# A transformer block on one Trainium2 core: a third seven-product pair in both column groups of the product behind the mixers, and a residual that enters the second group through PSUM

## The chip, the core and the metric

One Trainium2 chip, of which the kernel uses one core. The metric is the device time of one execution in microseconds (us), lower is better. The kernel is one launch and works in fp32; matrix products are made from split operands, as told below.

## The reference, cut to what matters

One layer on 256 rows of 2048 features. Two mixers, each with eight heads, work on one input projection; their results `y_sb` and `y_ca` go through a projection each, are gated and summed, and then comes the product that this document is about, `merged @ w_mix_out` with a residual. A gated feed-forward part (FFN) and a small gated addition follow.

```python
merged = (sigmoid(gate_sb) * (y_sb @ w_sb_out[i])
          + sigmoid(gate_ca) * (y_ca @ w_ca_out[i]))
x = x + merged @ w_mix_out[i]          # 256x2048 @ 2048x2048
h = rmsnorm(x, g_ffn[i])
g_ff, u_ff = split(h @ w_ffn_in[i], 2)
x = x + (silu(g_ff) * u_ff) @ w_ffn_out[i]
h = rmsnorm(x, g_ple[i])
x = x + sigmoid(h @ w_ple_gate[i]) * (p[i] @ w_ple_in[i])
out = rmsnorm(x, g_final)
```

## The kernel before, in words

**Split products.** Every operand of a product is held as two numbers, a rounded `hi` and the rest `lo`. A product of two 128-wide blocks is three matmuls of 128x512: hi by hi, hi by lo, lo by hi (`three`, L302 to 307). Activations lie in tables (T1, T2, T3), one 128-row block `kt` of features after the other, hi and lo halves behind each other. Weights come by DMA in pieces of 128x1024 (`raw`, issued by SP, L241); ScalarE (ACT) casts them to `hi` (L277), VectorE (DVE) subtracts to get `lo` (L257). There are five `raw` buffers, and two more from the place told below on; three buffers for `hi` and three for `lo`, later four.

**Units.** The product behind the mixers is made in two units (`unit`, L174), each of 16 feature blocks by two column blocks of 512: the first makes columns 0 to 1023, the second columns 1024 to 2047. In a unit the feature blocks go two and two, pair 0 to pair 7. A plain pair is two pieces, one for each column block, with 12 matmuls each, 24 in all. A pair named in `MIX_PAIRS` is one piece of 21 matmuls instead (`pair_products`, L312): seven products in place of eight, as in Strassen's and Winograd's scheme, on sums of the operands. Four of the seven go to banks of their own (`su`, the other half of PSUM); `mid` (L848) adds these up after the last such pair of a unit.

**What a seven-product pair needs.** Its weights are both column blocks' pieces at once. DVE makes three sums into `xf` and one in place in `raw` (four subtractions of 128x512), ACT casts `xf` to its hi half, DVE subtracts to get its lo half (128x1536); both halves lie in a room of T3 (`mix_rooms`). That is `split_pair` (L282). On the other side it needs a "form", four sums of 128x128 blocks of the table with hi and lo (`sums_of`, L462), made while the table is made; two forms fit in the tile FP.

**What comes ahead.** The two projections behind the mixers go before, on T2, which holds `y_sb` in its blocks 0 to 7 and `y_ca` in 8 to 15. When a column block of the second projection is complete, its gated sum (in `gates`) is transposed on TensorE (PE) and written to T1, four feature blocks at a time (`into_table`, L473). The last of these four steps runs when the first unit is already three pieces in. Then the memory of the attention stage is given up (`att.close`, `mid_stack.close`, L1007 and 1008), T3 and the two added `raw` buffers take the same place, and the four PSUM banks of the attention stage become the `su` banks of the first unit.

**After a unit.** `add_to_residual` (L962) adds, for each of the four 128x512 parts, PSUM to the sums from `mid`, and the result to the residual `x`: two DVE steps each. Units of the FFN's second product have another way, a `seed`: ACT copies the residual into the unit's PSUM banks before its first matmul (`seed_next`, L340), the matmuls accumulate on it, and one DVE step for each part writes `x` (`add_to_sums`, L1064).

**Order.** Each engine works its own instructions strictly in the program's order, which a scheduling layer fixes when the kernel is built. Pieces are split up to three ahead of the products. Whoever stands in an engine's order behind an instruction that waits, waits too.

Of the kernel before, what the change touches and what calls it, by code (L numbers as in the profile page):

```python
# [12 lines left out]
ALU = mybir.AluOpType  # L13
# [5 lines left out]
NT = 2  # L19
D = 2048  # L20
KD = D // P
# [10 lines left out]
NB = 512  # L32
# [1 line left out]
FF_BLOCKS = [12, 16, 16]  # L34

PAIRS = (2, 4, 6)
MIX_PAIRS = (4, 6)
OUT_PAIRS = {12: (2, 3, 4), 16: (2, 4, 5, 6)}
OUT_ORDERS = {
    12: ((0, 0, 1, 1, -2, 3, 3, -4, 5, 5), (0, 0, -2, 1, -3, 1, -4, 5, 5)),  # L40
# [12 lines left out]
def block_kernel(ctx: ExitStack, tc: tile.TileContext, x, p, w_in, w_sb_out, w_ca_out, w_mix_out,  # L53
# [18 lines left out]
    nc = tc.nc  # L72
# [13 lines left out]
    def aux(name):  # L86
        pool, width, tag = ps_ax[-1]
        return pool.tile([P, width], F32, tag=tag, name=name)
# [8 lines left out]
    T1 = bp.tile([P, KD, 2, S], F32R, tag="T1", name="T1")  # L97
    T2 = bp.tile([P, KD, 2, S], F32R, tag="T2", name="T2")
    x_ = bp.tile([P, NT, D], F32, tag="x", name="x")
    FP = bp.tile([P, 2, 2, 4, P], F32R, tag="FP", name="FP")  # L100
# [59 lines left out]
    def group(kind, wsrc, n0, kts, lhs, post, needs=lambda kt: None, row0=0, keep=None, after=None):  # L160

        ncol, nk = (NB, 2) if kind == "row" else (FB, 4)
        g = dict(kind=kind, post=post, lhs=lhs, ps=None, keep=keep, after=after)
        kts = list(kts)
        for j in range(0, len(kts), nk):
            part = kts[j : j + nk]
            r = (row0 + j) * P
            pieces.append(dict(
                g=g, kts=part, ncol=ncol, first=j == 0, last=j + nk >= len(kts),
                src=[wsrc[r : r + len(part) * P, n0 : n0 + ncol].rearrange("(k p) n -> p k n", p=P)],  # L170
                needs=[k for k in (needs(kt) for kt in part) if k is not None],
            ))

    def unit(wsrc, n0s, kts, lhs, forms, ext, slots, mid, post, needs, row0=0, pairs=PAIRS, alone=None, after=None,  # L174
             order=None, seed=None):


        if alone is None:
            state["unit"] = state.get("unit", -1) + 1
        pool = state["unit"] % 2 if alone is None else alone  # L180
        g = dict(kind="unit", post=post, mid=mid, slots=slots, after=after, lhs=lhs, keep=None, forms=forms, ext=ext, pool=pool,
                 side=1 - pool, hold=alone is not None, seed=seed)
        kts = list(kts)
        if order is None:
            order = [j for i in range(len(kts) // 2) for j in ([-i] if i in pairs and i < len(kts) // 2 - 1 else [i, i])]
        taken = [-i for i in order if i < 0]
        begun = set()
        for i in order:
            own = i < 0
            i = abs(i)  # L190
            part = kts[2 * i : 2 * i + 2]
            r = (row0 + 2 * i) * P
            src = [wsrc[r : r + 2 * P, n0 : n0 + NB].rearrange("(k p) n -> p k n", p=P) for n0 in n0s]
            pc = dict(g=g, kts=part, ncol=NB, needs=[needs(kt) for kt in part])
            if own:
                pieces.append(dict(pc, src=src, pair=True, first=i == taken[0], last=i == taken[-1]))
            else:
                b = int(i in begun)
                begun.add(i)
                pieces.append(dict(pc, src=[src[b]], block=b, first=i == 0, last=2 * i + 2 == len(kts)))  # L200
# [229 lines left out]
    def later(fn, n=3):  # L430

        for _ in range(n):
            tasks.append((None, lambda: None))
        tasks.append((None, fn))
# [38 lines left out]
    def into_table(dst, c, src, gain=None, key=None, forms=None, pool=None, pairs=PAIRS):  # L473


        n = ps_ax[-1][1] // S if pool is None else 2
        for k0 in range(0, 4, n):
            ps = (aux("tp") if pool is None else late["ps"][pool].tile([P, 512], F32, tag="mm", name="tp"))
            ps = ps.rearrange("p (k s) -> p k s", k=n)
            for k in range(n):  # L480
                for t in range(NT):
                    nc.tensor.transpose(ps[:, k, t * P : (t + 1) * P], src[:, t, (k0 + k) * P : (k0 + k + 1) * P], ident)  # L482
            step = n if forms is None else 2
            for k1 in range(0, n, step):
                table_part(dst, 4 * c + k0 + k1, ps[:, k1 : k1 + step, :], gain, forms, pairs)
        for k in range(4):
            done.add((key, 4 * c + k))

    def table_part(dst, kt, ps, gain, forms, pairs):
        n = ps.shape[1]  # L490
        ks = slice(kt, kt + n)
        g = None if gain is None else [gT[:, gain + kt + k : gain + kt + k + 1] for k in range(n)]
        if forms is not None and kt // 2 in pairs:
            af = state["work"]("af").rearrange("p (k s) -> p k s", k=2)
            if g is None:
                nc.scalar.copy(af, ps)
            else:
                for k in range(2):
                    nc.scalar.activation(af[:, k, :], ps[:, k, :], AF.Identity, scale=g[k])
            nc.scalar.copy(dst[:, ks, 0, :], af)  # L500
            minus(dst[:, ks, 1, :], af, dst.bitcast(F32)[:, ks, 0, :])
            sums_of(af, forms(kt))
        elif g is None:
            nc.scalar.copy(dst[:, ks, 0, :], ps)
            minus(dst[:, ks, 1, :], ps, dst.bitcast(F32)[:, ks, 0, :])
        else:
            for k in range(n):
                nc.scalar.activation(dst[:, kt + k, 0, :], ps[:, k, :], AF.Identity, scale=g[k])
                nc.vector.scalar_tensor_tensor(dst[:, kt + k, 1, :], ps[:, k, :], g[k], dst.bitcast(F32)[:, kt + k, 0, :],
                                               ALU.mult, ALU.subtract)  # L510
# [404 lines left out]
    x_ = bp.tile([P, NT, D], F32, tag="x", name="x")  # L915
# [7 lines left out]
    def out_post(m, c):  # L923
        def post(ps):
            cs = slice(c * NB, (c + 1) * NB)
            gt = gates[:, :, m, cs]
            for t in range(NT):
                by = rstd if (m, c) == (1, 0) else r1
                with tc.issue_after(state["cast"].ins):
                    nc.scalar.activation(gt[:, t, :], gt[:, t, :], AF.Sigmoid, scale=by["mix"][:, t : t + 1])  # L930
            for t in range(NT):
                nc.vector.tensor_tensor(gates[:, t, m, cs], ps[t], gates[:, t, m, cs], ALU.mult)
            if m == 1:
                mg = gates[:, :, 0, cs]
                nc.vector.tensor_tensor(mg, mg, gt, ALU.add)
                later(lambda: into_table(T1, c, mg, key="mg", forms=lambda kt: FP[:, kt // 4 - 2], pairs=MIX_PAIRS))
        return post

    for m, wo in ((0, w_sb_out), (1, w_ca_out)):
        for c in range(4):  # L940
            group("row", wo[0], c * NB, range(8 * m, 8 * m + 8), T2, out_post(m, c), needs=lambda kt: ("y", kt))
        state["places"] = 0
        flush(2.67 if m == 0 else 1, in_turn=m == 0)
# [13 lines left out]
    def C_slots():  # L957
        C = late["pool"].tile([P, 4, NB], F32, tag="C", name="C")
        late["C"] = C
        return [C[:, i, :] for i in range(4)]  # L960

    def add_to_residual(g, b, c):  # L962
        add_sums(g, b)
        for t in range(NT):
            xc = x_[:, t, c * NB : (c + 1) * NB]
            nc.vector.tensor_tensor(xc, xc, g["C"][2 * b + t], ALU.add)
# [10 lines left out]
    def mix_post(c0):  # L977
        def post(g, b):
            c = c0 + b
            add_to_residual(g, b, c)  # L980
            if b == 1:
                next_tables(late["T3"], c, 16, "ffn", g["pool"])
            residual_done(c, "ffn")
            if c == 3:
                tasks.append(("p2", lambda: broadcast(p2bc, p2, late["pool"])))
        return post
# [14 lines left out]

    mix_rooms = []
    for c in (0, 2):
        unit(w_mix_out[0], (c * NB, (c + 1) * NB), range(KD), T1, lambda kt: FP[:, kt // 4 - 2], mix_rooms, C_slots,
             mid, mix_post(c), lambda kt: ("mg", kt), pairs=MIX_PAIRS)
    flush(until=("mg", KD - 1))
    att.close()  # L1007
    mid_stack.close()
# [42 lines left out]
    def in_post(dst, c, key, pairs):  # L1051
# [8 lines left out]
            if b == 1:  # L1060
                hidden(dst, c, key, g, pairs)
        return post

    def add_to_sums(g, b, c):  # L1064
        for t in range(NT):
            nc.vector.tensor_tensor(x_[:, t, c * NB : (c + 1) * NB], g["ps"][2 * b + t], g["C"][2 * b + t], ALU.add)

    def residual_of(c0):
        return lambda b, t: x_[:, t, (c0 + b) * NB : (c0 + b + 1) * NB]

    def out_unit_post(c0, last):
        def post(g, b):
# [18 lines left out]
    for blk, nk in enumerate(FF_BLOCKS):  # L1091
        key = f"h{blk}"
        for c in range(nk // 4):
# [3 lines left out]
                 pairs=PAIRS if j else (), after=None if j else scale_next)  # L1097
# [124 lines left out]
```

## Time and profile before

| | us |
|---|---|
| median of 3 runs (1456.23 to 1456.53) | 1456.28 |
| the profiled execution, as a run | 1455.66 |
| its span in the profile | 1453.9 |
| PE busy in the span | 1443.5 |
| DVE busy | 1249.7 |
| ACT busy | 829.6 |

The span runs from the first to the last instruction; the run's time lies 1.8 us above it. Lines of the profile name the source line of the kernel before, the engine, the operation, and the tiles as output<-inputs. Matmuls overlap in the engine's pipeline, so that each has a duration of about 0.39 us but a new one starts every 0.23 us; the chain of waits shows the latter. The first of the two units runs from about 569 to 613 us, the second to about 657 us.

### The profile page before, as it was taken

Reading aid. Unit: us, or ns where it says so; the run is one execution under the profiler, and the core shown is the slowest. Engines: PE = TensorE matmul, PEld = TensorE weight load, DVE = VectorE, ACT = ScalarE, POOL = GpSimd, SP = SyncE. Lnnn points to the kernel's source line nnn. Section 1 sums busy time; section 2 is a strip of 40 time slices with the busy share of each in tenths; the row PEclk is TensorE's granted clock in tenths of the full one; section 3 lists DMA queues with packets and bytes.
Section 4 is the critical chain, followed back from the end, with each engine's and each line's share of the span. In section 5 each row is a group of like instructions: output and inputs, shape, how many; then the busy total and the mean of one; then the engine's idle time right before and its main releaser. Section 6 shows DMA issues by size and latency. Waiting matters only on the chain.

```text
span 1453.9 us, 18702 instructions
## 1 busy us (share of the span) xinstructions
PE 1443.5 (99%) x6837; PEld 1208.8 (83%) x6837; DVE 1249.7 (86%) x1587; ACT 829.6 (57%) x993; POOL 25.1 (2%) x44
## 2 busy tenths in 40 slices
PE   9999999999999999999999999999999999999997
PEld 7888888888888888888888888888888888888886
DVE  6979777898987767888999999999999989999785
ACT  6456555655545665555556655566655556666652
POOL 0200000000010000000000000000000000000100
PEclk9999999999999999999999999999999999999999
DMA  9866555666675655765666666666666666665871
GB/s 319 283 189 212 181 172 172 180 205 198 199 257 164 180 168 181 231 204 173 198 192 189 196 222 194 199 201 208 193 194 216 195 186 201 215 189 178 275 230 70
DMA packets 164731, 291.17 MB, mean 200 GB/s; under 512 B 9024, under 2 KB 42096, under 8 KB 164384
## 3 DMA queue, kind: packets, MB, share of 16 engines
q1 hardware_dynamic: 162528, 281.32, 62.0%
q0 software_dynamic: 2112, 8.68, 1.8%
q8 instruction: 53, 0.87, 0.2%
q14 instruction: 38, 0.31, 0.1%
HBM read 284.19 MB, written 5.77 MB: 199 GB/s over the span
## 4 chain that ended last, share of the span: by engine, by line
PE 96%; DVE 2%; DMA 1%; issue 1%; ACT 0%; DVEq 0%; SPq 0%; ACTq 0%
PE mm L307 67%; PE su L307 13%; PE mm L392 8%; PE mm L394 4%; PE tp L482 1%; DVE lo L257 1%; DMA raw<-in_w_in 1%; PE mml L307 0%; DMA raw<-in_w_ple_in 0%; PE mm L382 0%; PE xps L536 0%; DVE xf L257 0%; PE yp L709 0%; ACT hi L277 0%; PE wt L800 0%
## 5 line engine op out<-in xcount | busy, mean ns | idle before, releaser
L307 PE MATMUL mm<-hi,T 128*128 128x512 f32 x2650 | 854.6, 391 | 0.4 <-DVE v L854 0.4
L257 DVE TENSOR_TENSOR lo<-raw,hi 128x1024 fp32r<-128x1024 f32 (+1 forms) x517 | 625.1, 1221 | 121.9 <-ACT hi L277 113.0
L277 ACT CAST hi<-raw 128x1024 fp32r<-128x1024 f32 (+1 forms) x379 | 396.7, 1050 | 381.0 <-PE mm L307 257.8
L307 PEld LDWEIGHTS mm<-hi,T 128*128 128x128 f32 x2650 | 497.3, 188 | 103.0 <-issue 0.8
L307 PE MATMUL mm<-lo,T 128*128 128x512 f32 x1325 | 517.1, 391 | 0.0
L307 PEld LDWEIGHTS mm<-lo,T 128*128 128x128 f32 x1325 | 248.9, 188 | 50.7
L392 PE MATMUL mm<-T,hi 128*128 128x512 f32 x512 | 179.8, 398 | 0.0
L394 PE MATMUL mm<-T,lo 128*128 128x256 f32 x512 | 139.7, 280 | 0.0
L295 ACT CAST hi<-raw 128x1024 fp32r<-128x1024 f32 x69 | 72.7, 1053 | 76.2 <-DVE raw L257 29.5
L257 DVE TENSOR_TENSOR T<-xf,T 128x1536 fp32r<-128x1536 f32 x61 | 107.2, 1757 | 8.0 <-ACT T L298 7.2
L392 PEld LDWEIGHTS mm<-T,hi 128*128 128x128 f32 x512 | 94.6, 188 | 20.1
L257 DVE TENSOR_TENSOR xf<-raw 128x512 f32<-128x512 f32 x138 | 95.1, 689 | 13.2 <-DMA raw<-in_w_ffn_out 4.1
L394 PEld LDWEIGHTS mm<-T,lo 128*128 128x128 f32 x512 | 96.7, 189 | 2.3
L298 ACT CAST T<-xf 128x1536 fp32r<-128x1536 f32 x61 | 90.2, 1479 | 12.7 <-DVE xf L257 12.3
L292 ACT CAST hi<-raw 128x1024 fp32r<-128x1024 f32 x69 | 72.6, 1052 | 31.0 <-PE mm L307 20.5
L307 PE MATMUL mm<-T,T 128*128 128x512 f32 (+1 forms) x279 | 77.2, 371 | 0.0
L307 PE MATMUL su<-hi,T 128*128 128x512 f32 x170 | 66.1, 394 | 0.0
L307 PEld LDWEIGHTS mm<-T,T 128*128 128x128 f32 x279 | 49.3, 188 | 9.1
L854 DVE TENSOR_TENSOR C<-su,C 128x512 f32<-128x512 f32 x72 | 47.8, 686 | 0.4
L257 DVE TENSOR_TENSOR xf<-raw,xf 128x512 f32<-128x512 f32 x69 | 47.5, 689 | 0.5
L257 DVE TENSOR_TENSOR raw<-raw 128x512 f32<-128x512 f32 x69 | 47.5, 689 | 0.4
L307 PE MATMUL su<-T,FP 128*128 128x512 f32 x174 | 47.3, 389 | 0.0
(280 smaller groups left out, 1242.7 us busy)
## 6 DMA issues: line engine op xcount, KB each, us to landing
raw<-in_w_ffn_in SPq DMA_DIRECT2D x176, 512.0 KB, 4.1
raw<-in_w_in SPq DMA_DIRECT2D x160, 512.0 KB, 4.4
raw<-in_w_ffn_out SPq DMA_DIRECT2D x88, 512.0 KB, 4.4
raw<-in_w_mix_out SPq DMA_DIRECT2D x32, 512.0 KB, 4.6
raw<-in_w_ple_gate SPq DMA_DIRECT2D x32, 512.0 KB, 4.9
raw<-in_w_sb_out SPq DMA_DIRECT2D x16, 512.0 KB, 3.8
raw<-in_w_ca_out SPq DMA_DIRECT2D x16, 512.0 KB, 4.5
x<-in_x SPq DMA_DIRECT2D x4, 512.0 KB, 10.2
```

What stands on the lines that cost most here:

```text
L257: return nc.vector.tensor_tensor(out, a, b, ALU.subtract)
L277: state["cast"] = nc.scalar.copy(hi[:, c : c + m], raw[:, c : c + m])
L292: nc.scalar.copy(h1, raw1)
L295: nc.scalar.copy(h2, raw2)
L298: nc.scalar.copy(xh, xf)
L307: state["mm"] = nc.tensor.matmul(ps, u, v, start=first, stop=last, skip_group_check=True)
L392: nc.tensor.matmul(ps, hi[:, i, f], lhs[:, kt, :, :].rearrange("p c s -> p (c s)"), start=a, stop=False)
L394: nc.tensor.matmul(ps[:, :S], lo[:, i, f], lhs[:, kt, 0, :], start=False, stop=z)
L482: nc.tensor.transpose(ps[:, k, t * P : (t + 1) * P], src[:, t, (k0 + k) * P : (k0 + k + 1) * P], ident)
L854: nc.vector.tensor_tensor(C[i], q, C[j], ALU.add)
```

## The change

Pair 2 becomes a seven-product pair in both units (`MIX_PAIRS`). Its form needs a third place, and lies where T2 holds the blocks 0 and 1 of `y_sb`, which only the first projection reads (`F_mix`). The second unit is seeded with the residual, so that `add_to_sums` follows it in place of `add_to_residual`; the two helpers move up in the file, unchanged. A pair whose number is in the list is taken as one piece in the order 0, 0, 1, 1, -2, 3, 3, -4, 5, 5, -6, 7, 7 (a minus marks the one piece); before, pair 2 stood there as 2, 2.

```diff
--- before.py
+++ after.py
@@ -34,7 +34,7 @@
 FF_BLOCKS = [12, 16, 16]
 
 PAIRS = (2, 4, 6)
-MIX_PAIRS = (4, 6)
+MIX_PAIRS = (2, 4, 6)
 OUT_PAIRS = {12: (2, 3, 4), 16: (2, 4, 5, 6)}
 OUT_ORDERS = {
     12: ((0, 0, 1, 1, -2, 3, 3, -4, 5, 5), (0, 0, -2, 1, -3, 1, -4, 5, 5)),
@@ -933,9 +933,10 @@
             if m == 1:
                 mg = gates[:, :, 0, cs]
                 nc.vector.tensor_tensor(mg, mg, gt, ALU.add)
-                later(lambda: into_table(T1, c, mg, key="mg", forms=lambda kt: FP[:, kt // 4 - 2], pairs=MIX_PAIRS))
+                later(lambda: into_table(T1, c, mg, key="mg", forms=lambda kt: F_mix[kt // 4 - 1], pairs=MIX_PAIRS))
         return post
 
+    F_mix = [T2.rearrange("p k c s -> p (k c s)")[:, :1024].rearrange("p (c f s) -> p c f s", c=2, f=4), FP[:, 0], FP[:, 1]]
     for m, wo in ((0, w_sb_out), (1, w_ca_out)):
         for c in range(4):
             group("row", wo[0], c * NB, range(8 * m, 8 * m + 8), T2, out_post(m, c), needs=lambda kt: ("y", kt))
@@ -959,6 +960,13 @@
         late["C"] = C
         return [C[:, i, :] for i in range(4)]
 
+    def add_to_sums(g, b, c):
+        for t in range(NT):
+            nc.vector.tensor_tensor(x_[:, t, c * NB : (c + 1) * NB], g["ps"][2 * b + t], g["C"][2 * b + t], ALU.add)
+
+    def residual_of(c0):
+        return lambda b, t: x_[:, t, (c0 + b) * NB : (c0 + b + 1) * NB]
+
     def add_to_residual(g, b, c):
         add_sums(g, b)
         for t in range(NT):
@@ -977,7 +985,10 @@
     def mix_post(c0):
         def post(g, b):
             c = c0 + b
-            add_to_residual(g, b, c)
+            if g["seed"] is None:
+                add_to_residual(g, b, c)
+            else:
+                add_to_sums(g, b, c)
             if b == 1:
                 next_tables(late["T3"], c, 16, "ffn", g["pool"])
             residual_done(c, "ffn")
@@ -1001,8 +1012,8 @@
 
     mix_rooms = []
     for c in (0, 2):
-        unit(w_mix_out[0], (c * NB, (c + 1) * NB), range(KD), T1, lambda kt: FP[:, kt // 4 - 2], mix_rooms, C_slots,
-             mid, mix_post(c), lambda kt: ("mg", kt), pairs=MIX_PAIRS)
+        unit(w_mix_out[0], (c * NB, (c + 1) * NB), range(KD), T1, lambda kt: F_mix[kt // 4 - 1], mix_rooms, C_slots,
+             mid, mix_post(c), lambda kt: ("mg", kt), pairs=MIX_PAIRS, seed=residual_of(c) if c else None)
     flush(until=("mg", KD - 1))
     att.close()
     mid_stack.close()
@@ -1060,13 +1071,6 @@
             if b == 1:
                 hidden(dst, c, key, g, pairs)
         return post
-
-    def add_to_sums(g, b, c):
-        for t in range(NT):
-            nc.vector.tensor_tensor(x_[:, t, c * NB : (c + 1) * NB], g["ps"][2 * b + t], g["C"][2 * b + t], ALU.add)
-
-    def residual_of(c0):
-        return lambda b, t: x_[:, t, (c0 + b) * NB : (c0 + b + 1) * NB]
 
     def out_unit_post(c0, last):
         def post(g, b):
```

The rows that follow are the built programs' orders, with source lines of each program's own file. Names carry buffer numbers. First DVE before, at the end of the first unit's last table step (`work` and FP: the form of pair 6) and its first seven-product pair, pair 4 (`xf_5194`, weights `raw_5132` and `raw_5134`):

```order
L257 TENSOR_TENSOR lo_5145<-raw_5059,hi_5144 128x1024
L257 TENSOR_TENSOR FP_74<-work_4224,FP_74 128x512
L257 TENSOR_TENSOR lo_5196<-raw_5132,hi_5195 128x1024
L257 TENSOR_TENSOR lo_5165<-raw_5061,hi_5164 128x1024
L257 TENSOR_TENSOR xf_5194<-raw_5134 128x512
L257 TENSOR_TENSOR raw_5134<-raw_5134,raw_5132 128x512
L257 TENSOR_TENSOR xf_5194<-raw_5134 128x512
L257 TENSOR_TENSOR xf_5194<-raw_5132,xf_5194 128x512
L257 TENSOR_TENSOR lo_5198<-raw_5134,hi_5197 128x1024
L257 TENSOR_TENSOR lo_5226<-raw_5136,hi_5225 128x1024
L257 TENSOR_TENSOR T3_5123<-xf_5194,T3_5123 128x1536
```

Now the same engine after. The first seven-product pair is pair 2 (`xf_5141`, weights `raw_5062` and `raw_5064`):

```order
L257 TENSOR_TENSOR lo_5143<-raw_5062,hi_5142 128x1024
L257 TENSOR_TENSOR lo_5145<-raw_5064,hi_5144 128x1024
L466 TENSOR_TENSOR work_4224<-work_4224 128x128
L257 TENSOR_TENSOR work_4224<-work_4224 128x128
L257 TENSOR_TENSOR T1_71<-tp_5100,T1_71 128x2x256
L257 TENSOR_TENSOR T1_71<-work_4224,T1_71 128x2x256
L257 TENSOR_TENSOR work_4224<-work_4224 128x128
L257 TENSOR_TENSOR lo_5157<-raw_5066,hi_5156 128x1024
L257 TENSOR_TENSOR work_4224<-work_4224 128x128
L257 TENSOR_TENSOR lo_5211<-raw_5135,hi_5210 128x1024
L257 TENSOR_TENSOR FP_74<-work_4224,FP_74 128x512
L257 TENSOR_TENSOR T3_5126<-xf_5141,T3_5126 128x1536
```

The four sums of pair 2 have moved ahead of these rows, and its last step, the lo half in T3, stands right behind the form of pair 6 (FP), four rows behind a piece of pair 3 (`lo_5157`); before, four weight pieces and four sums stood between that form and the first lo half in T3.

ACT before at the same place, with the names of the engines and DMA queues whose semaphores each row waits for (`DMAHW` and `DMASW` are queues):

```order
L277 CAST hi_5144<-raw_5059 128x1024 [waits DMAHW4_49,DVE_49,PE_49]
L470 CAST FP_74<-work_4224 128x512 [waits DVE_49]
L292 CAST hi_5195<-raw_5132 128x1024 [waits DMAHW6_49,PE_49]
L277 CAST hi_5164<-raw_5061 128x1024 [waits DMASW5_49,DMASW4_49,DMASW6_49,DMASW3_49,DMASW7_49,DMASW0_49,DMAHW5_49,DVE_49,Pool_49]
L295 CAST hi_5197<-raw_5134 128x1024 [waits DMAHW2_49,DVE_49,PE_49]
L277 CAST hi_5225<-raw_5136 128x1024 [waits DMAHW7_49,PE_49]
L298 CAST T3_5123<-xf_5194 128x1536 [waits DVE_49]
```

ACT after:

```order
L277 CAST hi_5156<-raw_5066 128x1024 [waits DMAHW4_49,DVE_49,PE_49]
L292 CAST hi_5210<-raw_5135 128x1024 [waits DMAHW6_49,DVE_49,PE_49]
L470 CAST FP_74<-work_4224 128x512 [waits DVE_49]
L298 CAST T3_5126<-xf_5141 128x1536 [waits DMASW4_49,DMASW5_49,DMASW3_49,DMASW6_49,DMASW0_49,DMASW7_49,DVE_49,Pool_49]
L277 CAST hi_5178<-raw_5068 128x1024 [waits DMAHW5_49]
L295 CAST hi_5212<-raw_5137 128x1024 [waits DMAHW2_49,DVE_49,PE_49]
```

The cast of `xf` into T3 was the fifth row behind the form of pair 6 (FP) and is now the next one. T3 lies in memory that the attention stage held, and the first ACT row that writes to that memory carries the waits for those who used it last, DVE (the FP row above, which reads `work`) and the DMAs: `hi_5164` before (a fourth `hi` buffer in that memory), the T3 cast after.

PE after, from pair 4's first weight piece (`hi_5210`) on; `su2` and `su3` are banks for the own products of pair 2, `T3_5126` its sums, `T2_72` its form:

```order
L307 MATMUL su0_5182<-hi_5210,T1_71 128x512
L307 MATMUL mm0_5048<-hi_5210,T1_71 128x512
L307 MATMUL su0_5182<-lo_5211,T1_71 128x512
L307 MATMUL su0_5182<-hi_5210,T1_71 128x512
L307 MATMUL mm0_5048<-lo_5211,T1_71 128x512
L307 MATMUL mm0_5048<-hi_5210,T1_71 128x512
L307 MATMUL su2_5184<-T3_5126,T2_72 128x512
L307 MATMUL su3_5185<-T3_5126,T2_72 128x512
L307 MATMUL mm1_5049<-T3_5126,T1_71 128x512
L307 MATMUL mm0_5074<-hi_5178,T1_71 128x512
L307 MATMUL mm1_5075<-hi_5178,T1_71 128x512
L307 MATMUL su2_5184<-T3_5126,T2_72 128x512 x2
```

The first matmuls that read T3's hi half stand ahead of `hi_5178` (pair 3), and those that read its lo half two rows further on. Between the eight transposes of the last table step and the first of them stand 34 matmuls; 39 ahead of the first that reads the lo half, and 64 ahead of the first that reads `lo_5213` (pair 4's second weights).

## The prediction

> **What bounds the kernel now.** I read the page first, for the engines' busy time and the chain that ended last.
>
> ```profile
> PE 1443.5 (99%) x6837; PEld 1208.8 (83%) x6837; DVE 1249.7 (86%) x1587; ACT 829.6 (57%) x993; POOL 25.1 (2%) x44
> PE 96%; DVE 2%; DMA 1%; issue 1%; ACT 0%; DVEq 0%; SPq 0%; ACTq 0%
> ```
>
> PE is the bound over the whole span. The waits of PE are next: these three rows are all that the view lists.
>
> ```profile
> PE warm L580 <- POOL mhalf L108: 1.2, 1, 1.2
> PE mm L307 <- DVE v L854: 0.4, 1, 0.4
> PE mm L382 <- ACT hi L277: 0.3, 1, 0.3
> ```
>
> None lies in the two units of this change, so a matmul taken away there is worth its full spacing, as long as its cover holds. The chain of waits from 568 to 622 us gives the spacing:
>
> ```profile
> 568.83 9.52 PE mm L307 x42
> 578.36 0.87 PE tp L482 x8
> 579.23 10.46 PE mm L307 x46
> ...
> 608.55 12.47 PE mm L307 x55
> ```
>
> 12.47 / 55 = 0.227 us for a matmul. The busy time by stretch (columns: stretch, length, then PE, PEld, DVE, ACT, POOL, the granted clock, DMA share, GB/s) shows what is next to PE:
>
> ```profile
> 587.00:593.00 6.00, 6.00 (x28) 4.95 (x27) 3.56 (x6) 1.44 (x2) 0.00 (x0) 1.00 0.77 268
> 593.00:599.00 6.00, 6.00 (x28) 4.92 (x27) 6.00 (x5) 3.84 (x4) 0.00 (x0) 1.00 0.68 210
> 617.00:623.00 6.00, 6.00 (x32) 5.06 (x31) 6.00 (x8) 4.48 (x10) 0.00 (x0) 1.00 0.52 154
> ```
>
> DVE has no idle time from the first seven-product pair of the first unit on (593 us). Between the units (617 us) it has none either. PE keeps going there because DVE is ahead. How far ahead decides this change.
>
> **The change part by part.**
>
> *Matmuls.* A plain pair has 24, a seven-product pair 21, and two pairs change: 6 x 0.227 = 1.36 us off PE. TensorE: Matmul & The Clock Gate of the Trainium skill (Back-to-back issue gap) gives about 131 ns for sustained matmuls of 512 columns; by that the saving would be an estimated 0.8 us and my time 0.6 us higher. The chain row above is this kernel's own, and I use it.
>
> *Work of the two pairs on DVE and ACT.* These are groups of the page:
>
> ```profile
> L257 DVE TENSOR_TENSOR lo<-raw,hi 128x1024 fp32r<-128x1024 f32 (+1 forms) x517 | 625.1, 1221 | 121.9 <-ACT hi L277 113.0
> L257 DVE TENSOR_TENSOR T<-xf,T 128x1536 fp32r<-128x1536 f32 x61 | 107.2, 1757 | 8.0 <-ACT T L298 7.2
> L257 DVE TENSOR_TENSOR xf<-raw 128x512 f32<-128x512 f32 x138 | 95.1, 689 | 13.2 <-DMA raw<-in_w_ffn_out 4.1
> L298 ACT CAST T<-xf 128x1536 fp32r<-128x1536 f32 x61 | 90.2, 1479 | 12.7 <-DVE xf L257 12.3
> L854 DVE TENSOR_TENSOR C<-su,C 128x512 f32<-128x512 f32 x72 | 47.8, 686 | 0.4
> ```
>
> Each pair adds four sums and a lo half on DVE, 4 x 0.689 + 1.757 = 4.5 us, and 1.5 us on ACT. The cover is DVE's idle time and its lead; where these end, it costs PE time.
>
> *The third form.* Here is DVE in order of time (start, length, what), before that step and when it makes a form of the same kind:
>
> ```profile
> 564.57 1.23 DVE L257 TENSOR_TENSOR lo<-raw,hi 128x1024 fp32r<-128x1024 f32 x1 [1.39 <-ACT hi L277]
> ...
> 568.39 0.28 DVE L466 TENSOR_TENSOR work<-work 128x128 f32<-128x128 f32 x1
> ...
> 573.87 0.68 DVE L257 TENSOR_TENSOR FP<-work,FP 128x512 fp32r<-128x512 f32 x1
> ```
>
> 4 x 0.28 + 0.68 = 1.8 us more for DVE around 557 to 564 us, where idle stretches of 1.4 us stand in front of pieces: nothing on PE. Without that cover it would be those 1.8 us.
>
> *The seed.* It trades DVE steps for ACT copies in the second unit:
>
> ```profile
> L966 DVE TENSOR_TENSOR x<-x,C x8: 682/687/691, 612.4 to 660.4; 128x512 f32<-128x512 f32 x8
> L348 ACT COPY mm<-x x24: 572/587/593, 779.8 to 1315.5; 128x512 f32<-128x512 f32 x24
> ```
>
> Four of the first go (2.7 us of DVE at the second unit's end), four of the second come (2.3 us of ACT). The seeds wait for `mid`, DVE work that runs while PE does pair 7, 24 x 0.227 = 5.4 us. Nothing on PE; if `mid` came late, up to these 2.3 us.
>
> *The new order of the first unit.* Here I expect the cost. The seven-product work starts right behind the last table step, and its sums go to T3, whose memory is free only when FP, that step's last operation, is done. Before, with the same operations in time (PE, ACT, DVE, then SP's DMA issue):
>
> ```profile
> 575.24 0.39 PE L307 MATMUL mm<-hi,T 128*128 128x512 f32 x1
> 578.19 1.03 PE L482 MATMUL tp<-ident,gates 128*128 128x128 f32 x8
> 578.99 0.48 PE L307 MATMUL mm<-lo,T 128*128 128x512 f32 x1
> 579.30 0.39 PE L307 MATMUL mm<-hi,T 128*128 128x512 f32 x1
> ...
> 594.29 0.40 PE L307 MATMUL mm<-lo,FP 128*128 128x512 f32 x1
> ```
>
> ```profile
> 575.67 1.05 ACT L277 CAST hi<-raw 128x1024 fp32r<-128x1024 f32 x1 [2.12 <-PE mm L307]
> 584.28 1.05 ACT L292 CAST hi<-raw 128x1024 fp32r<-128x1024 f32 x1 [1.15 <-PE mm L307]
> ```
>
> ```profile
> 582.65 1.23 DVE L257 TENSOR_TENSOR lo<-raw,hi 128x1024 fp32r<-128x1024 f32 x1 [0.40 <-ACT hi L277]
> 583.79 0.68 DVE L257 TENSOR_TENSOR FP<-work,FP 128x512 fp32r<-128x512 f32 x1
> 585.37 2.36 DVE L257 TENSOR_TENSOR lo<-raw,hi 128x1024 fp32r<-128x1024 f32 x2 [0.89 <-ACT hi L292]
> 590.06 0.69 DVE L257 TENSOR_TENSOR xf<-raw 128x512 f32<-128x512 f32 x1 [2.33 <-DMA raw<-in_w_mix_out]
> ...
> 592.85 2.35 DVE L257 TENSOR_TENSOR lo<-raw,hi 128x1024 fp32r<-128x1024 f32 x2
> ```
>
> ```profile
> 584.62 0.37 SPq L241 DMA_DIRECT2D raw<-in_w_mix_out  x1
> raw<-in_w_mix_out SPq DMA_DIRECT2D x1, 512.0 KB, 4.2
> raw<-in_w_mix_out SPq DMA_DIRECT2D x1, 512.0 KB, 5.4
> ```
>
> (The last two are issues at 583.9 and 584.6 us, with their time to landing.) The transposes stay where they are, 38 matmuls into the unit in both orders. The matmuls behind them start at 578.99, 579.30, and from there every 0.227 us. I call that count k.
>
> 1. `hi_5210` waits until PE has left `hi_5142`, at k = 18: start 579.30 + 17 x 0.227 = 583.16, end 0.39 later, 583.55. Its cast starts 0.04 us behind that (575.24 + 0.39 against 575.67) and ends at 583.59 + 1.05 = 584.64.
> 2. `lo_5211` follows 0.04 later, starts at 584.68 and, as at 582.65 and 583.79, lets FP start 1.14 us later, at 585.82, to end at 586.50. It was 584.47 before: FP is now queued behind that piece.
> 3. ACT can cast the sums into T3 only now: 586.55 to 588.03. PE wants them at k = 34, 579.30 + 33 x 0.227 = 586.79. It waits 1.25 us. Behind that matmul in PE's order everything waits.
> 4. The lo half ends at 588.08 + 1.76 = 589.84; PE wants it at k = 39, 587.93, now 589.2. Another 0.65 us, 1.9 in sum.
> 5. The same FP frees the added `raw` buffers. Their DMA goes out 0.15 us later (584.47 to 584.62), 586.65, and lands after 4.2 to 5.4 us, 590.85 to 592.05. From there it was 4.0 us (590.06 to 592.85 + 1.22) to the end of that pair's second lo half: 594.9 to 596.1. PE wants it at k = 64, 593.6, or 595.5 with the wait so far. So the waits end at 1.9 to 2.5 us in sum.
>
> I take 2.2 us, between these two ends. The step was hardly covered before: the lo half in question ended at 592.85 + 1.22 = 594.07, and PE took it (`mm<-lo,FP`) at 594.29. For bounds I widen: if T3 was free earlier, only point 5 is left, with 594.9 - 593.6 = 1.3 us; if `lo_5157`, `su0` and pair 6 are late too (leads of 0.1 to 1.3 us in the same reckoning), 3.5 us.
>
> *Sum.* -1.36 + 2.2 = +0.8 us. The profiled execution, 1455.66 us (span 1453.9), becomes 1456.5. It lies 0.6 us below the median of the runs, 1456.28, from which I forecast 1457.1.
>
> **The rivals.**
>
> *The cover holds.* DVE's queue and the DMA come out better than I reckon, or T3's memory isn't held by FP; PE never waits, and the time is 1456.28 - 1.36 = 1454.9 us. For it: PE has no wait in all of 569 to 629 us with DVE full. Against it: FP's place in the queue, and a lead of only 0.2 us at the same step.
>
> *The two units collide.* Between the last seven-product pair of the first unit and the first of the second, PE now has pair 7, 0 and 1, 72 x 0.227 = 16.3 us. DVE has `mid` (4 x 0.686), eight steps of `add_to_residual` (8 x 0.687), two pieces of pair 1, four sums and one lo half of the new pair: 2.7 + 5.5 + 2.4 + 2.8 + 1.2 = 14.6 us. It fits by 1.7. If the weights of that pair land late by one 4.2 us transfer, PE waits 2.5 us more: 1459.6 us, slower. It decides once the landing is over 1.7 us late.
>
> *PE's clock falls.* The clock at the program's end, in stretches of 1 us (same columns as above):
>
> ```profile
> 1445.00:1446.00 1.00, 0.38 (x4) 0.18 (x2) 0.07 (x1) 0.56 (x2) 0.00 (x0) 1.00 0.00 0
> 1447.00:1448.00 1.00, 0.00 (x0) 0.00 (x0) 0.60 (x4) 0.65 (x3) 0.00 (x0) 0.87 0.00 0
> 1448.00:1449.00 1.00, 0.00 (x0) 0.00 (x0) 1.00 (x4) 0.56 (x1) 0.00 (x0) 0.50 0.00 0
> ```
>
> PE stops at 1445.4, and the clock is halved from 1447.74 on (0.87 is 0.74 at full and 0.26 at half): 2.4 us of idleness were enough. An unbroken wait of that length would halve it; if it stays so for as long again, that adds 1.2 us, and with 3.5 us of waits the time is 1456.28 - 1.36 + 3.5 + 1.2 = 1459.6 us. My waits are broken into 1.25, 0.65 and up to 0.6 with matmuls between, so it should not happen. The same page of the Trainium skill (HAM clock gate) says half rate after an idle window of about 3.4 us: by that it takes still more than I allow, and the window's phase could explain the 2.4 here.
>
> **How the numbers follow.** A measurement of this kernel can tell about 0.2% from no change, 2.9 us: faster is below 1453.4, slower above 1459.2. My forecast has 0.63, with 1456.2 to 1458.4 us by the bounds of the wait; the cover holds 0.2; the units collide 0.1; the clock falls 0.05; the rest, 0.02, is something that I don't see, put as faster. Slower by over 0.2% are most of the last two rivals: 0.12. Faster needs more than the 1.36 us that there are: 0.02. The range goes from just under the second case to just under the slow ones, 1454.8 to 1458.9, with some 0.16 outside.
>
> **What would show it.** Right: in the profile after, PE waits for ACT's cast L298 into T3 at 587 us and for DVE soon after, some 2 us in sum, then none; FP's last write ends at about 586.5; the DMA of the added `raw` goes out 0.15 us later. PE's busy matmuls are six fewer. Wrong: no wait of PE there; or waits between the units at 615 to 635 us; or a granted clock under 1.00 at 587 to 600 us.

## The result, and the profile after

The changed kernel takes 1457.93 us (median of 22 runs, 1456.49 to 1459.64), the kernel before 1456.18 us beside it (22 runs, 1455.19 to 1457.59). The ratio is 1.0012, with a 95% interval of 1.0006 to 1.0017: 0.9 to 2.5 us slower, 1.75 by the medians. 1457.1 was forecast, 0.8 us over the kernel before.

The profiled execution took 1457.36 us (span 1455.7). Its busy time and its chain by engine, from the page:

```profile
PE 1443.5 (99%) x6831; PEld 1206.7 (83%) x6831; DVE 1256.2 (86%) x1598; ACT 835.3 (57%) x1001; POOL 25.1 (2%) x44
PE 92%; DVE 4%; DMA 2%; issue 1%; ACT 0%; SPq 0%; DVEq 0%; ACTq 0%
```

PE has six matmuls fewer and is no less busy. DVE and DMA are on the chain for 4% and 2%; they were 2% and 1%. All waits of PE that the view lists:

```profile
PE warm L580 <- POOL mhalf L108: 1.2, 1, 1.2
PE su L307 <- ACT T L298: 1.0, 1, 1.0
PE mm L307 <- DVE v L854: 0.9, 1, 0.9
PE mm L382 <- ACT hi L277: 0.3, 1, 0.3
PE mm L307 <- DVE lo L257: 0.2, 1, 0.2
```

New are the second and the last. The last lies in the first 100 us of the program and the third in attention code, neither of which the change touches; the third was 0.4 before, and in the kernels below it is 0.5 to 1.0 us. That is noise of a size that matters here, and so I compare profiles from the start of the last table step's eight transposes on (`PE L482 MATMUL tp`, 578.19 us before, 578.72 after) to the end of the span: 1453.9 - 578.19 = 875.7 us before, 1455.7 - 578.72 = 877.0 after, 1.3 more.

Where they go is seen in PE's order of time in the first unit (start, length, what):

```profile
586.23 0.39 PE L307 MATMUL mm<-hi,T 128*128 128x512 f32 x1
586.49 0.50 PE L307 MATMUL su<-lo,T 128*128 128x512 f32 x1
586.83 0.40 PE L307 MATMUL su<-hi,T 128*128 128x512 f32 x1
...
587.29 0.40 PE L307 MATMUL mm<-hi,T 128*128 128x512 f32 x1
588.64 0.73 PE L307 MATMUL su<-T,T 128*128 128x512 f32 x2 [0.95 <-ACT T L298]
589.21 0.40 PE L307 MATMUL mm<-T,T 128*128 128x512 f32 x1
589.59 0.73 PE L307 MATMUL mm<-hi,T 128*128 128x512 f32 x2
590.44 1.20 PE L307 MATMUL su<-T,T 128*128 128x512 f32 x4
591.48 0.62 PE L307 MATMUL mm<-T,T 128*128 128x512 f32 x2
```

From 586.23 to 591.48 there are 14 matmuls, for which 14 x 0.227 = 3.18 us are needed, and 5.25 pass: 2.07 us lost. That is more than the view's 1.0, which lists one wait here and leaves out the short ones. ACT and DVE beside it:

```profile
584.12 1.05 ACT L292 CAST hi<-raw 128x1024 fp32r<-128x1024 f32 x1 [0.76 <-PE su L307]
...
587.12 1.47 ACT L298 CAST T<-xf 128x1536 fp32r<-128x1536 f32 x1 [1.42 <-issue]
```

```profile
585.21 1.23 DVE L257 TENSOR_TENSOR lo<-raw,hi 128x1024 fp32r<-128x1024 f32 x1 [0.38 <-ACT hi L292]
586.35 0.69 DVE L257 TENSOR_TENSOR FP<-work,FP 128x512 fp32r<-128x512 f32 x1
588.62 1.76 DVE L257 TENSOR_TENSOR T<-xf,T 128x1536 fp32r<-128x1536 f32 x1 [1.58 <-ACT T L298]
```

FP ends at 587.04 and the cast into T3 starts at 587.12, after 1.42 us of idleness, though its input `xf` had been complete since 578.98. Most of the rest is at the boundary of the units. The chain of waits (start, length, what) leads there from a weight transfer, and PE's order of time behind it follows:

```profile
587.18 4.78 DMA raw<-in_w_mix_out
...
606.21 7.15 DMA raw<-in_w_mix_out
...
628.13 2.37 DVE lo L257 x2
```

```profile
629.85 0.63 PE L307 MATMUL mm<-hi,T 128*128 128x512 f32 x2
630.54 0.50 PE L307 MATMUL mm<-lo,T 128*128 128x512 f32 x1
```

The transfer of 606.21 lands 7.15 us later; DVE works without a break from there to 630.50, and PE takes what it made 0.04 us later. By the spacing that matmul was due at 629.85 + 2 x 0.227 = 630.30, and so it is 0.24 us late, a wait that the view leaves out. That the late transfer is the cause is read from the chain; no run below takes it away.

### The profile page after: what moved, and what is told of

Its sections match the earlier page's. It is cut to its first block, busy times and chain, and to the rows that moved or that the text cites. A ratio compares the mean times of both kernels' runs of the same rounds, so it can differ in the third digit from the quotient of the medians.

```text
span 1455.7 us, 18711 instructions
## 1 busy us (share of the span) xinstructions
PE 1443.5 (99%) x6831; PEld 1206.7 (83%) x6831; DVE 1256.2 (86%) x1598; ACT 835.3 (57%) x1001; POOL 25.1 (2%) x44
## 4 chain that ended last, share of the span: by engine, by line
PE 92%; DVE 4%; DMA 2%; issue 1%; ACT 0%; SPq 0%; DVEq 0%; ACTq 0%
PE mm L307 64%; PE su L307 12%; PE mm L392 8%; PE mm L394 4%; DVE lo L257 2%; PE tp L482 1%; DMA raw<-in_w_mix_out 1%; DMA raw<-in_w_in 1%; DMA raw<-in_w_ple_in 1%; DVE xf L257 1%; PE mml L307 0%; DVE T L257 0%; PE xps L536 0%; DVE raw L257 0%; PE yp L709 0%
## 5 line engine op out<-in xcount | busy, mean ns | idle before, releaser
L307 PE MATMUL mm<-hi,T 128*128 128x512 f32 x2626 | 848.1, 391 | 0.9 <-DVE v L854 0.9
L277 ACT CAST hi<-raw 128x1024 fp32r<-128x1024 f32 (+1 forms) x375 | 392.6, 1050 | 366.9 <-PE mm L307 247.5
L307 PEld LDWEIGHTS mm<-hi,T 128*128 128x128 f32 x2626 | 492.5, 188 | 103.1 <-issue 1.2
L307 PE MATMUL mm<-lo,T 128*128 128x512 f32 x1313 | 512.2, 390 | 0.1
L307 PEld LDWEIGHTS mm<-lo,T 128*128 128x128 f32 x1313 | 246.6, 188 | 50.8 <-DVE lo L257 0.5
L257 DVE TENSOR_TENSOR T<-xf,T 128x1536 fp32r<-128x1536 f32 x63 | 110.4, 1753 | 9.0 <-ACT T L298 8.5
L295 ACT CAST hi<-raw 128x1024 fp32r<-128x1024 f32 x71 | 74.8, 1053 | 71.3 <-DVE raw L257 30.3
L298 ACT CAST T<-xf 128x1536 fp32r<-128x1536 f32 x63 | 93.2, 1479 | 14.8 <-DVE xf L257 12.6
L292 ACT CAST hi<-raw 128x1024 fp32r<-128x1024 f32 x71 | 74.7, 1052 | 32.3 <-PE mm L307 18.8
L307 PE MATMUL mm<-T,T 128*128 128x512 f32 (+1 forms) x285 | 79.6, 372 | 0.0
L307 PE MATMUL su<-hi,T 128*128 128x512 f32 x178 | 68.7, 393 | 0.0
L307 PEld LDWEIGHTS mm<-T,T 128*128 128x128 f32 x285 | 50.3, 188 | 9.3
L307 PE MATMUL su<-T,FP 128*128 128x512 f32 x174 | 47.4, 389 | 0.0
```

Of the source, the lines that this page charges most:

```text
L257: return nc.vector.tensor_tensor(out, a, b, ALU.subtract)
L277: state["cast"] = nc.scalar.copy(hi[:, c : c + m], raw[:, c : c + m])
L292: nc.scalar.copy(h1, raw1)
L295: nc.scalar.copy(h2, raw2)
L298: nc.scalar.copy(xh, xf)
L307: state["mm"] = nc.tensor.matmul(ps, u, v, start=first, stop=last, skip_group_check=True)
```

## The experiments

All are timed against the kernel before on the same chip. The last three columns come from each run's profile: the span, the start of the transposes, and the rest behind it.

| run | median | before beside it | ratio, 95% interval | span | transposes | rest |
|---|---|---|---|---|---|---|
| before | 1456.18 | | | 1453.9 | 578.19 | 875.7 |
| after | 1457.93 | 1456.18 | 1.0006 to 1.0017 | 1455.7 | 578.72 | 877.0 |
| e1, after again | 1457.62 | 1456.42 | 1.0000 to 1.0017 | 1457.7 | 578.63 | 879.1 |
| e2, sums in T2 | 1459.83 | 1456.42 | 1.0014 to 1.0031 | 1458.9 | 579.25 | 879.7 |
| e3, second unit alone | 1456.78 | 1456.42 | 0.9994 to 1.0012 | 1454.6 | 578.76 | 875.8 |
| e4, first unit alone | 1458.26 | 1456.42 | 1.0006 to 1.0024 | 1456.5 | 579.32 | 877.2 |
| e5, step's tile kept | 1455.60 | 1456.60 | 0.9987 to 1.0004 | 1452.9 | 578.14 | 874.8 |
| e6, the same in before | 1456.10 | 1456.60 | 0.9988 to 1.0005 | 1454.1 | 578.45 | 875.7 |
| e7, no seed | 1457.96 | 1456.60 | 1.0001 to 1.0019 | 1457.0 | 579.20 | 877.8 |
| e8, e5 without seed | 1457.17 | 1456.60 | 0.9993 to 1.0011 | 1453.8 | 578.36 | 875.4 |
| e9, transfer early | 1457.02 | 1456.19 | 0.9997 to 1.0015 | 1454.7 | 578.23 | 876.5 |
| e10, sums in T2, in turn | 1457.48 | 1456.19 | 0.9999 to 1.0017 | 1454.3 | 578.18 | 876.1 |
| e11, e5 again | 1455.72 | 1456.19 | 0.9986 to 1.0003 | 1454.2 | 578.89 | 875.3 |

Each profile is that of one run: it is the fastest of the eleven in `e5`, `e8` and `e10`, and the slowest in `e1`.

### Which unit, and the same kernel a second time

`e1` is the changed kernel unedited.

> The changed kernel itself, beside the others on one chip. All theories: about 1.2 to 1.8 us over the kernel before (it was 1.75 over in the result). In its profile PE waits at about 588.6 us for ACT's cast L298 into T3 (1.0 us in the first profile), some 2 us in sum in the first unit, and little or nothing at the boundary of the units. The scatter of the runs is of interest: if the excess at the boundary (0.33 us in the first profile, behind a weight transfer of 7.15 us) varies from run to run, the runs of this kernel spread more than those of before.

It came out 1.2 us over the kernel before, and its profile shows 3.4 us more from the transposes on. The wait for the cast is the same to a tenth, but another one follows. Its chain of waits has these two transfers, and its PE takes pair 4's second weights so:

```profile
587.09 6.06 DMA raw<-in_w_mix_out
...
607.40 8.00 DMA raw<-in_w_mix_out
```

```profile
595.24 0.39 PE L307 MATMUL mm<-hi,T 128*128 128x512 f32 x1
595.84 0.50 PE L307 MATMUL mm<-hi,FP 128*128 128x512 f32 x1 [0.22 <-ACT hi L295]
596.18 0.40 PE L307 MATMUL su<-hi,FP 128*128 128x512 f32 x1
596.79 0.50 PE L307 MATMUL mm<-hi,T 128*128 128x512 f32 x1 [0.21 <-ACT hi L277]
597.30 0.50 PE L307 MATMUL mm<-lo,FP 128*128 128x512 f32 x1
597.64 0.40 PE L307 MATMUL mm<-hi,FP 128*128 128x512 f32 x1
597.88 0.40 PE L307 MATMUL su<-lo,FP 128*128 128x512 f32 x1
```

From 595.24 to 597.88 six matmuls start, 6 x 0.227 = 1.36 us of work in 2.64: 1.28 lost. In the first profile these went out every 0.23 us. The difference is the landing of the added `raw` buffer's transfer, 6.06 us against 4.78. Two kernels below, with the same first unit, agree: in `e7` it took 5.91 us, and 1.1 us are lost at the same matmuls (six starts in 2.45 us from 595.85 on); in `e4`, where the two transfers issued there took 4.5 us by the median, nothing is lost. Of the 3.4 us, -1.36 + 2.07 + 1.28 = 2.0 are so accounted for; the other 1.4 lie at the boundary, behind a transfer of 8.00 us, and in small steps.

`e3` has three pairs only in the second unit (the first hunk), `e4` only in the first and no seed (the second):

```diff
-mid, mix_post(c), lambda kt: ("mg", kt), pairs=MIX_PAIRS, seed=residual_of(c) if c else None)
+mid, mix_post(c), lambda kt: ("mg", kt), pairs=MIX_PAIRS if c else (4, 6), seed=residual_of(c) if c else None)
```

```diff
-mid, mix_post(c), lambda kt: ("mg", kt), pairs=MIX_PAIRS, seed=residual_of(c) if c else None)
+mid, mix_post(c), lambda kt: ("mg", kt), pairs=(4, 6) if c else MIX_PAIRS)
```

> The third pair and the seed in the second unit alone; the first unit has its two pairs as before. My theory (all of the cost lies in the first unit): three matmuls saved and no new wait, 1456.2 - 0.7 = 1455.5 us, with 0.3 more where the boundary of the units is late. Rival (the cost lies in the second unit, its seed or the boundary): 1457 to 1458 us.

> The third pair in the first unit alone; the second unit has its two pairs and no seed, as before. My theory (all of the cost lies in the first unit): three matmuls saved and the wait of about 2 us there, 1456.2 - 0.7 + 2.0 = 1457.5 us, up to 1458. Rival (the cost lies in the second unit or the seed): 1455.5 us.

`e4` has the loss (1.8 us over the kernel before, expected 1.3 to 1.8) and the wait for L298 of 1.0 us. `e3` has no wait in the first unit, and is still level with the kernel before, where 0.7 us less was expected: three matmuls' gain is spent, part of it in a wait of 0.2 us for DVE at the boundary. So the loss is the first unit's; the second unit and the boundary together lose about what their three matmuls gain.

### One release that holds two things

`e2` takes the sums out of T3:

```diff
-mix_rooms.append(T3.rearrange("p k c s -> p (k c s)")[:, 5120:])
+mix_rooms.append(T2.rearrange("p k c s -> p (k c s)")[:, 1024:4096])
```

> The sums' hi and lo halves go to a free part of T2 instead of T3, in both units; nothing else is edited, FP stays where it is in DVE's queue and the added raw buffers still wait for it. My theory (T3's memory is held by FP's operand until FP is done): the wait of PE for the cast L298 at 588.6 us goes, about 1.3 to 2 us; what is left is the six matmuls' gain, less a wait for lo_5213, whose transfer still goes out behind FP: 0 to 1.3 us. So 1455.0 to 1456.3 us where before is 1456.2, 1.5 us below the changed kernel. Rival (the cost is DVE and ACT being full: the pair's additions themselves are late, wherever they are written): the wait stays, and the time with it, 1457.9. Rival (the cost lies at the boundary of units or in the seed): the same time as the changed kernel, 1457.9, though the first unit's wait is gone.

The wait at 588 us went, and the kernel became 3.4 us slower than before, against my theory as I had put it. With the sums free, the planner moved their lo half ahead of the table step on DVE, so that FP came later. Its DVE order (the lo half, the step's first operation, FP), the chain of waits, PE, and the clock by stretch (columns as in the prediction):

```profile
582.55 1.75 DVE L257 TENSOR_TENSOR T<-xf,T 128x1536 fp32r<-128x1536 f32 x1
584.22 0.28 DVE L466 TENSOR_TENSOR work<-work 128x128 f32<-128x128 f32 x1
...
588.60 0.69 DVE L257 TENSOR_TENSOR FP<-work,FP 128x512 fp32r<-128x512 f32 x1
```

```profile
589.42 4.67 DMA raw<-in_w_mix_out
```

```profile
594.33 0.39 PE L307 MATMUL mm<-hi,T 128*128 128x512 f32 x1
596.71 0.50 PE L307 MATMUL mm<-hi,FP 128*128 128x512 f32 x1 [1.99 <-ACT hi L295]
```

```profile
594.00:596.00 2.00, 0.72 (x4) 0.26 (x2) 1.82 (x3) 0.39 (x1) 0.00 (x0) 1.00 0.87 302
596.00:598.00 2.00, 1.07 (x3) 0.48 (x3) 1.97 (x3) 2.00 (x3) 0.00 (x0) 1.00 0.03 11
598.00:599.00 1.00, 0.99 (x5) 0.70 (x5) 1.00 (x2) 1.00 (x2) 0.00 (x0) 1.00 0.79 154
599.00:600.00 1.00, 1.00 (x4) 0.81 (x3) 1.00 (x2) 1.00 (x2) 0.00 (x0) 0.50 0.99 303
...
602.00:603.00 1.00, 1.00 (x5) 0.81 (x4) 1.00 (x1) 0.00 (x0) 0.00 (x0) 0.79 0.97 330
```

FP ends at 589.29, 2.2 us later than in the changed kernel (1.7 counted from the transposes), the transfer goes out behind it, and PE waits 1.99 us for pair 4's second weights. Then the clock is halved from 599.0 to 602.4 us; in PE's order of time ten matmuls take 3.88 us from 598.97 on, for which 2.27 are needed, 1.6 lost. So FP holds two things, T3's memory and the transfer, and the second alone is enough to cost time. `e9` and `e10` let go one each. `e9` gives the first added buffer the place of a value tile that had been freed long before, and leaves PE's and DVE's order here as it is:

```diff
-return mp.tile([P, NT, NB], F32, tag=f"v{i}", name="v")
+return (bp if i == 0 else mp).tile([P, NT, NB], F32, tag=f"v{i}", name="v")
-work = mp.tile([P, 1024], F32, tag="v0", name="work")
+work = mp.tile([P, 1024], F32, tag="qT0", name="work")
-more_places(lambda: lp.tile([P, 1024], F32, tag="raw", name="raw", bufs=MORE), MORE)
+def added():
+    state["added"] = state.get("added", 0) + 1
+    if state["added"] % 2:
+        return bp.tile([P, 1024], F32, tag="v0", name="raw")
+    return lp.tile([P, 1024], F32, tag="raw", name="raw")
+more_places(added, MORE)
```

> Only one of the two things that FP holds is let go: the first added raw buffer takes the place of the value tile v0, in the pool that stays, and its transfer goes out long before FP; T3's memory and the second added raw buffer are held by FP as in the changed kernel, and DVE's and PE's order in this stage is the changed kernel's. My theory (either hold alone costs about as much as both, since both end with FP): the wait for the cast L298 stays (steps of 1.35, 0.38 and 0.5 us at 588 to 591 us, 2.0 us with the restarts), there is none for hi_5212 and lo_5213 at 595 to 598 us whatever the transfers take, and the time is 1456.4 - 1.36 + 2.0 + 0.3 = 1457.3 us; its runs spread less than the changed kernel's 3 us. Rival (the late transfer is the cost, and the cast's wait only lies in front of it): 1455.5 us.

PE in `e9`, at the cast and at pair 4's second weights:

```profile
588.16 0.73 PE L307 MATMUL su<-T,T 128*128 128x512 f32 x2 [0.96 <-ACT T L298]
...
595.07 0.39 PE L307 MATMUL mm<-hi,FP 128*128 128x512 f32 x1
595.30 0.39 PE L307 MATMUL su<-hi,FP 128*128 128x512 f32 x1
```

As expected: the wait for the cast is there, none follows, 1457.02 us where 1457.3 was expected. Its runs lie within 1.8 us (1456.21 to 1458.03), those of the changed kernel within 3.2; but those of `e5`, where both holds are gone, within 2.8, so that the late transfer isn't shown to make the spread. `e10` is `e2` with the lo half of the first pair's sums queued behind FP's last operation, which `sums_of` keeps in `state["form"]`:

```diff
-minus(f[:, 1], fm, f.bitcast(F32)[:, 0])
+state["form"] = minus(f[:, 1], fm, f.bitcast(F32)[:, 0])
...
-minus(xl, xf, xh.bitcast(F32))
+if rooms is mix_rooms and not state.get("first"):
+    state["first"] = True
+    with tc.issue_after(state["form"].ins):
+        minus(xl, xf, xh.bitcast(F32))
+else:
+    minus(xl, xf, xh.bitcast(F32))
```

> The other hold alone is let go: the sums' halves go to a free part of T2, and the first of their lo halves is queued behind FP on DVE, so that FP is not pushed back by it; the added raw buffers are held by FP. FP stands one weight piece earlier than in the changed kernel, so its transfer should go out at about 585.9 us and land at 590.4 to 592. My theory: no wait for the cast at 588 us; PE wants hi_5212 at about 593.8, and gets it 3.2 us behind the landing (two sums' and the cast's time), 593.6 to 595.2: a wait of 0 to 1.8 us by what the transfer took, and 1455.3 to 1457.0 us. Rival (the late transfer is nothing by itself): no wait there and 1455.2 us.

Its chain of waits, and its PE (L314 here is L307 there):

```profile
585.30 5.27 DMA raw<-in_w_mix_out
```

```profile
592.70 0.39 PE L314 MATMUL mm<-hi,T 128*128 128x512 f32 x1
593.26 0.50 PE L314 MATMUL mm<-hi,FP 128*128 128x512 f32 x1 [0.17 <-ACT hi L297]
593.60 0.40 PE L314 MATMUL su<-hi,FP 128*128 128x512 f32 x1
594.21 0.49 PE L314 MATMUL mm<-hi,T 128*128 128x512 f32 x1 [0.21 <-ACT hi L277]
```

No wait for the cast, but one for these weights, as `e1` has it, after a landing of 5.27 us. The profiled execution took 1456.14 us, within the 1455.3 to 1457.0 expected; it is the fastest run, and the median of 1457.48 is above them, for a reason that the profile can't show. On the same chip `e9` and `e10` are 1.3 and 1.8 us above `e11`, which lets go both holds.

`e5` frees both, and `e11` is `e5` a second time: the step's tile moves to the pool that stays, and FP holds nothing.

```diff
-return mp.tile([P, NT, NB], F32, tag=f"v{i}", name="v")
+return (bp if i == 0 else mp).tile([P, NT, NB], F32, tag=f"v{i}", name="v")
-work = mp.tile([P, 1024], F32, tag="v0", name="work")
+work = bp.tile([P, 1024], F32, tag="v0", name="work")
```

> The value tile v0, whose place the step's work tile takes, lies in the pool that stays instead of the one that is closed; so neither T3's memory nor the added raw buffers wait for FP. The planner brings the cast into T3 ahead of pair 6's last form and the added raw transfer goes out behind the transposes, about 6 us earlier. My theory (FP holds both): the waits in the first unit go altogether, and what is left is the six matmuls' gain less some tenths at the boundary of the units: 1456.3 - 1.36 + 0.3 = 1455.2 us, 2 to 3 us below the changed kernel. Rival (DVE and ACT are too full for the third pair in the first unit): a wait of 1 to 2 us on DVE or ACT stays between 583 and 600 us and the time stays at 1457 to 1458. Rival (the cost lies between the units or in the seed): the first unit is clean and the time still over 1456.5.

> The kernel before with the same move of the value tile: what the move does without the third pair. My theory (the kernel before had no wait there to lose): 1456.3, within 0.3 us of the kernel before. Rival (the move brings a gain of its own, by earlier transfers or a better order): below 1455.8.

> The kernel with the value tile in the pool that stays, once more, beside the two that let go one hold each. My theory (both holds gone): 1.0 us below the kernel before, 1455.4 us, and below either of the other two by as much as their waits. Rival (the 1.0 us of the first measurement was chance): level with the kernel before, 1456.4.

ACT, DVE and PE in `e5`:

```profile
580.25 1.50 ACT L298 CAST T<-xf 128x1536 fp32r<-128x1536 f32 x1
```

```profile
589.01 0.69 DVE L257 TENSOR_TENSOR FP<-work,FP 128x512 fp32r<-128x512 f32 x1
```

```profile
584.26 0.62 PE L307 MATMUL su<-T,T 128*128 128x512 f32 x2
```

The cast is now 8.8 us ahead of FP, which itself comes later than in the changed kernel and disturbs nobody; DVE is as busy as there (1256.5 us against 1256.2). The view lists no wait of PE behind 570 us, and in `e11` one of 0.2, at the boundary. The rest is 874.8 us, 0.9 below the kernel before, of which the move by itself gives nothing by its profile (`e6`, 875.7). By the runs `e5` and `e11` are 1.0 and 0.5 us below the kernel before, and `e6` is 0.5 below as well. The intervals of `e5` and `e11` end below that of the changed kernel as first measured (that of `e1` begins at 1.0000), and all three take in 1. So the waits and their loss are gone, but a gain over the kernel before isn't shown, and still less that it comes from the third pair.

### The seed

`e7` leaves the seed out of the changed kernel, `e8` out of `e5`:

```diff
-mid, mix_post(c), lambda kt: ("mg", kt), pairs=MIX_PAIRS, seed=residual_of(c) if c else None)
+mid, mix_post(c), lambda kt: ("mg", kt), pairs=MIX_PAIRS)
```

> The changed kernel without the seed: the second unit adds its residual on DVE, as the kernel before. My theory (the seed is worth nothing on PE): within 0.5 us of the changed kernel, 1457.0 to 1458.2. Rival (the seed's copies on ACT, which stand ahead of casts, cost the tenths at the boundary of units): 0.3 to 0.8 us faster than the changed kernel, and no wait at 630 us. Rival (the seed is what pays for the third pair in the second unit): 1 us slower or more.

> The move of the value tile, three pairs in both units, no seed: the same question about the seed where the first unit is clean. My theory: within 0.5 us of the run with the move and the seed, about 1455.2. Rival (the seed costs at the boundary): 0.3 to 0.8 us below that run. Rival (the seed pays): 0.5 us or more above it.

`e7` is level with the changed kernel (1.36 us over the kernel before), as expected. `e8` is 1.6 us above `e5`. That is what the rival gave by which the seed pays; but their intervals overlap, both profiles are of the fastest run, and of the 0.6 us between their rests 0.4 are a wait at 851 us, in the FFN. Whether the seed pays something in the clean version stays open.

## Why the prediction was right, and what it missed

All times after lie 0.52 us later than the steps say, because that profile's first unit starts so much later.

1. **`hi_5210`.** Its cast was to end at 584.64; it ended at 585.17, which is 584.65 less the shift. Right.
2. **FP.** Forecast 586.50, measured 587.04 (586.52). Right.
3. **The cast into T3.** Forecast 586.55 to 588.03, measured 587.12 to 588.59. PE's wait was to be 1.25 us; the matmul came 588.64 - 587.29 = 1.35 us after the one ahead, 1.1 more than 0.227. Right.
4. **The lo half.** Forecast to end at 589.84, measured 588.62 + 1.76 = 590.38 (589.86). Both waits were put at 1.9 us, and 2.07 were lost. Part of that is a restart, which I hadn't priced: behind each matmul that waited here, the next one starts 0.34 us later instead of 0.227 (586.49 to 586.83). There are four of these from 586.49 to 591.48; without them 2.07 - 4 x 0.11 = 1.63 us are left. So the order and the cause are right, and that the sum comes so close is in part luck.
5. **The added transfer.** The cause is shown by `e9` and `e10`; its size failed. I let it land after 4.2 to 5.4 us, and two executions of the same kernel took 4.78 and 6.06. The first hid behind points 3 and 4, the second cost 1.28 us more. The upper end of 2.5 us for all waits should have been 2.07 + 1.28 = 3.3, near the 3.5 that I had as a bound for other reasons. The kernel before already had longer landings of the same size, issued in the windows 585.0 to 585.2 and 594.0 to 594.3 us:

```profile
raw<-in_w_mix_out SPq DMA_DIRECT2D x1, 512.0 KB, 6.3
raw<-in_w_mix_out SPq DMA_DIRECT2D x1, 512.0 KB, 6.2
```

**The sum.** Forecast -1.36 + 2.2 = +0.8; the profile's rest gives +1.3, the second profile's +3.4, the runs +1.75, with an interval of 0.9 to 2.5: the forecast of +0.8 lies just below it. The term that was mis-sized is that of the waits: point 5, and the boundary of the units, for which the sum had nothing.

**The rival of the colliding units** had the right place, a late weight transfer between the units (7.15 and 8.00 us), and the wrong form. I gave it as all or nothing, 2.5 us behind a slack of 1.7; it took some tenths in most profiles and up to 1.4 us in `e1`. Waits between the units at 615 to 635 us were one of my signs of being wrong, and the first profile has one, of 0.24 us.

**The cover holds** was wrong, and **the clock** stayed full in the changed kernel, as forecast; this row covers the waits:

```profile
587.00:593.00 6.00, 4.94 (x19) 3.13 (x19) 3.85 (x5) 2.42 (x2) 0.00 (x0) 1.00 0.69 224
```

**The third form and the seed** at nothing on PE: `e7` agrees; where everything else is clean, it stays open. **The six matmuls** as 1.36 us of gain fit `e5`: 0.9 us less rest, with some 0.3 us of short steps at the boundary.

## What to carry over

When a new step writes to memory that an older stage gives up, find the last operation that still uses it, and look at everything that is held by the same release: here one 0.7 us subtraction held a cast and a transfer, and taking away one hold showed the other. Moving the small tile that kept the pool open was worth more than the place of the sums. Price a transfer that has just lost its lead by the slowest landing of its size that the trace lists, not by those of its neighbours. Count the starts of the matmuls against their spacing: a list of waits leaves out the short ones and the restarts.

## What the runs showed of the hardware

- **A restart.** Behind a matmul that waited, the next one starts 0.34 us later where the spacing is 0.227: at 586.49 and 588.64 us in the changed kernel, at 595.84 in `e1`, at 596.71 in `e2`, 0.11 us for each interruption.
- **The clock after a short wait.** In `e2` PE stood still for 1.99 us up to 596.71, and was busy for 1.07 + 0.99 = 2.06 us of the four from 595 to 599 (the 0.72 in the row of 594 end at 594.72). The clock fell to half at 599.0, when PE had been at work again for over 2 us, and stayed there for 3.4 us (0.79 in the row of 602 is half speed to 602.4). TensorE: Matmul & The Clock Gate of the Trainium skill (Part 1, What's actually happening) has a free-running window of about 3.4 us, and half rate after at least one idle window. The length of the half-rate stretch agrees; but no 3.4 us were idle here. Nor does the phase of such a window explain the 2.4 us of idleness at the program's end, as the prediction offers: a window without work would need at least 3.4. The stop of 1.99 us is the only long one nearby and so the likely cause, which no run tests by itself. The runs fit: nine of the eleven of `e2` have a mean granted clock of 0.997, as its profile has, and of the changed kernel's 22 only the slowest. In the changed kernel 2.07 us lost in pieces left the clock at full. Two of the eleven runs of `e10` have 0.997 too, its two slowest, so that such a fall may be part of its high median.
- **Landing times.** One and the same transfer of 512 KB took 4.78 and 6.06 us in two executions of the changed kernel, 5.27 in `e10` and 4.67 in `e2`, and another 7.15 and 8.00. In the first unit the difference of the first two made 1.28 us, nearly as much as the six matmuls save.
